# One core, two transformer blocks: the expert loop at the very end, the shift products beside the gate-up, the bias strip behind the gates, and the first projection from features that are not yet normed

## The chip, the cores and the metric

The kernel runs on one core of a Trainium2 chip. The metric is the device time of one execution in microseconds. Each kernel has a few timed runs, and one further execution is recorded by the hardware profiler; the rows below are of that execution.

## The reference, cut to what matters

The input is one sequence of 512 tokens with 1024 features in float32. Two blocks follow each other.

```python
# first block
h = rms_norm(x, g_mix)                      # x * rsqrt(mean x^2) * g
proj = h @ w_in                             # conv parts, q, k, v, iq, ik, iw, two gates
score = sum_h iw[t,h] * relu(iq[t,h] . ik[s])   # index scores, causal
idx = top_k(score, 128)                     # 128 keys for each query
logits = q.k * 64**-0.5 + rel_bias[bucket(t - s)]   # on the chosen keys
x = x + (sigmoid(g_a) * y_conv + sigmoid(g_b) * y_attn) @ w_out
x = x + (silu(h2 @ w_gate) * (h2 @ w_up)) @ w_down
x = rms_norm(x, g_final)
# second block
sh1, sc1, gt1, sh2, sc2, gt2 = split(silu(c) @ ada_w + ada_b)
h = rms_norm(x, g1) * (1 + sc1) + sh1
z = h @ w_in_2                              # latent q and kv, rope key, conv, gates
... latent attention, 31 tap convolution, gates, x = x + gt1 * y
h = rms_norm(x, g2) * (1 + sc2) + sh2
x = x + gt2 * moe(h)                        # 32 experts, 2 for each token
out = rms_norm(x, g_final_2)
```

## The kernel before

Activations stand with features on the partitions: x is 8 blocks (k = 0 to 7) of 128 features by 512 tokens. Nearly all matmuls are float32 products made from a high and a low part: `split` writes the high part on ScalarE and the rest on VectorE or GpSimd. `dense` (L351) runs a weight matrix chunk by chunk. For a chunk SyncE loads `raw` (512 KB, 8 blocks of 128 by 128), ScalarE makes `wh` (L338), GpSimd makes `wl` (L339), TensorE runs 24 matmuls (`mm3`: high by high, high by low, low by high for the 8 blocks) into one of three PSUM buffers `mm`, and an evacuation function takes the result. `raw`, `wh` and `wl` come from one ring of nine buffers. `dense` is a generator; `next(g)` emits one step, so other work is emitted between chunks. The order in each engine's queue is fixed when the program is built: a planner places the instructions by its own estimate of their times, with the order of emission as priority. An engine runs its queue in order, and SyncE issues its DMAs in order.

**First projection.** `w_qk` has ten chunks: index key (m = 0), index queries (1 to 4), key (5), queries (6 to 9). The first NDEF = 5 read `xg`, the features times `g_mix` without the norm, and `ev_qk` multiplies their products with the norm factor `r`, spread over the partitions (L511). Then `norm_h` (L499) makes all 8 blocks of `h` (L502, and a split whose low part is made by VectorE for even k and by GpSimd for odd k). `w_vi` (v and the index weights iw, 72 columns) and the chunks m = 5 to 9 read `h`. Scores (L549) for one query block and one index head are two matmuls, a relu on ScalarE and a multiply-add on VectorE, and are emitted four at a time between the chunks. `w_cv` (12 chunks) and the gates (`w_ga`, `w_gb`) read `h` as well. The top-k tasks (L562) run beside `w_cv`, `w_ga` and `w_ya`.

**Bias strip.** The bias by distance stands in DRAM as `bd` (8 by 640); one DMA writes from it `bt` (8 by 128 by 512, 2 MB, DRAM to DRAM, L645), emitted behind the last `w_cv` chunk. The attention reads it one head at a time (`st<-bt`, L766).

**Ada and shift.** The 48 loads of `ada` are reduced on VectorE, one scaled addition of 128 by 512 for each half (`ada`, L704), one task beside each chunk of the first half of gate-up and of down, two beside each chunk of the second gate-up half until the 54 tasks are used up. `shift` (L902) takes for each of the six chunks of `w_lat` a load of 512 KB, eight VectorE operations of 128 by 128 (L905, L907), one matmul with a column of ones (L909) and a copy. It runs beside the first six of the eight `w_dn` chunks of the second half (L964), where rope tables and masks are also made.

**Experts.** Seventeen tiles of rows (seq) go through the experts; sixteen of 112 rows and one of 64. Rows of tiles 0 to 14 are added to `acc` in DRAM by indirect DMAs, those of the last two (i = 15 and 16) stay on the chip and are placed with one-hot matmuls (`keep_on_chip`, `place`). `loop` (L1725) is a `tc.For_i(1, ntl)` loop for further tiles with a count read from `ei`. Here its count is one, so no iteration runs: the trace has 17 gathers. It is emitted inside the tile sequence at i = LOOP = 16, ahead of `turn(16)` and `finish(16)`. After it `fin` (4 blocks of tokens) is read from `acc`, `place` adds the kept rows, ScalarE sums the squares, and the last norm and the output follow.

Of the kernel before, what the change touches and what calls it, by code (L numbers as in the profile page):

```python
# [19 lines left out]
P = 128  # L20
# [29 lines left out]
FM = "ppss"  # L50
FQ = 1
KS = 0
NDEF = 5
SE = 0
CB = 48
FAR = 512.0
# [17 lines left out]
GA1 = (0, 0, 0, 1, 0, 1, 0, 1, 1, 0)  # L74
NW = 9
NCH = 2
LOOP = 16
LF = True
NX = 18
NR = 8  # L80
# [158 lines left out]
def build(tc, A, out, taps=None):  # L239
# [57 lines left out]
    def vcol(n, j, w=1):  # L297
        o = V1[n] + j
        return vec[:, o:o + w]
# [196 lines left out]
    next(g)  # L496
    h = []

    def norm_h():  # L499
        for k in range(DB):  # L500
            t = blk("t")
            STT(t, x[k], vcol("g_mix", k), r, ALU.mult, ALU.mult)  # L502
            a = pair_of("h")
            split(t, *a, eng=G if k % 2 else V)
            h.append(a)


    def ev_qk(m, ps):
# [15 lines left out]

    next(g)
    next(g)
    norm_h()
    go(g)
    g = dense("w_qk", DB, h, ev_qk, src=A["w_qk"][NDEF:], m0=NDEF)


    wh, wl = wsplit(wload(A["w_vi"].rearrange("p k c -> p (k c)"), 576), 576)
    ps = psum("mm", "vi")
    mm3(ps[:72], wh, wl, 0, DB, h, M=72)
    vi = blk("t")
    act(vi[:72], ps[:72], ACT.Copy)
    ps = psum("tp")
    for b in range(NB):
        nc.tensor.transpose(ps[:, b * 72:(b + 1) * 72], vi[:72, b * P:(b + 1) * P], ident[:72, :72])
# [40 lines left out]

    scores = Tasks(*[(score, b, i) for b in range(1, NB) for i in range(8)])
    scores.run(SC[0])
    go(g, lambda i: scores.run(SC[1]))
    scores.run(SC[2])
    tops = Tasks(*[(topk, b, j) for j in range(16) for b in range(1, NB)])

# [52 lines left out]
    def beside(i):  # L639
        scores.run(SC[3])  # L640
        if not scores.ts:
            tops.run(TOP)

    go(dense("w_cv", DB, h, ev_cv), beside)
    nc.sync.dma_start(bt, bass.AP(tensor=bd.tensor, offset=bd.offset + 127,  # L645
                                    ap=[[640, 8], [-1, P], [1, S]]))


    gts = {}
# [3 lines left out]
        act(t, ps, ACT.Sigmoid, bias=vcol("b_gate", m))  # L653
        gts[m] = t

    mA = []

    def ev_ya(m, ps):
        t = blk("mA")
        TT(t, ps, gts[m], ALU.mult)  # L660
        mA.append(t)

    ga, ya = dense("w_ga", DB, h, ev_ga), dense("w_ya", 4, chl, ev_ya)
    for _ in range(NGA):
        next(ga)
        tops.run(3)
        next(ya)
        tops.run(1)
    tops.run(99)

    gd = {}
# [227 lines left out]

    shc = kpool.tile([P, NL], F32, name="shc")  # L900

    def shift(c):  # L902
        raw = wload(A["w_lat"][c].rearrange("p m k c -> p (m k c)"), D)
        t = blk("t")[:, :P]
        TS(t, raw[:, :P], adac[:, :1], None, ALU.mult)  # L905
        for k in range(1, DB):
            STT(t, raw[:, k * P:(k + 1) * P], adac[:, k:k + 1], t, ALU.mult, ALU.add)  # L907
        ps = psum("lg", "shift")
        mm(ps[:, :1], t, one1[:, :1])  # L909
        act(shc[:, c:c + 1], ps[:, :1], ACT.Copy)  # L910

    shifts = Tasks(*[(shift, c) for c in range(NL)])


    gs1 = kpool.tile([P, 8], F32, name="gs1")
# [3 lines left out]
    for half in range(2):  # L919
        hid = []  # L920
        st = {}

        def ev_gu(m, ps):
            t = blk("t")
            if m % 2 == 0:
                TT(t, ps, r, ALU.mult)
                act(t, t, ACT.Silu)  # L927
                G.tensor_tensor(t, t, r, ALU.mult)  # L928
                st["g"] = t
            else:  # L930
                TT(t, ps, st["g"], ALU.mult)
                a = pair_of("h" if len(hid) < NH else "h1" if len(hid) < NH1 else "hid")
                split(t, *a)
                hid.append(a)

        if half == 0:
            with soon(1):
                r = rstd_of(ssq.done(), out=blk("m2"))
        if half == 0:
            keep(act(cact, vcol2("c", 0, 8), ACT.Silu))  # L940
            keep(G.tensor_copy(trib, cst[:, 256:384]))
            G.tensor_copy(tri2[:, :32], cst[:32, 256:288])
            G.tensor_tensor(tri2[:, 32:], cst[:32, 256:288], cst[:32, :32], ALU.add)
            G.tensor_copy(moeb, moec[:, 88:328])
            G.memset(oneb, 1.0)
        go(dense("w_gu", DB, h, ev_gu, src=A["w_gu"][half * 22:(half + 1) * 22]),
           lambda i: adas.run(AD[2 * half]))

        def ev_d(m, ps):
            TT(x[m], ps, x[m], ALU.add)  # L950
            if half:
                a = pair_of("xg")
                split(x[m], *a, scale=gs1[:, m:m + 1])
                xg.append(a)
                s1.add(x[m])
                s2.add(x[m], scale=vcol("g_final", m))

        if half:
            STT(gs1, adac[:, 8:16], 1.0, vcol2("norm1_g", 0, 8), ALU.add, ALU.mult)
            TT(gs1, gs1, vcol("g_final", 0, 8), ALU.mult)  # L960
            rt = rope_tables()
            mk = masks()
        go(dense("w_dn", 11, hid, ev_d, src=A["w_dn"][half]),
           lambda i: shifts.run(1) if half else adas.run(AD[2 * half + 1]))  # L964


    KQ = 96
# [754 lines left out]
        ohs.append(oh)  # L1722
        ys.append((yh, yl))

    def loop():  # L1725
        for j in range(LOOP + 1, 17):
            weights(j, LF)

        ntl = nc.values_load(ei[0:1, 16:17], min_val=1, max_val=16)
        with tc.For_i(1, ntl) as t:  # L1730
            st = mr[0].tile([P, 4], F32, name="lsl")[:, :3]

            nc.sync.dma_start(slots[16 * P:].rearrange("(g p) c -> p g c", p=P), slt[:, 16:])
            nc.sync.dma_start(st[:64], slots[bass.ds(16 * P + 64 * t, 64)])
            ix = mr[0].tile([P, 1], I32, name="lix")
            V.tensor_copy(ix[:64], st[:64, 0:1])
            w = further(t)
            xg = gather(xgb[0], ix, 64)
            scaled(64, xg, st)
            down(w, turned(64, hidden(w, features(64, xg, xtb), st)), yb[0])  # L1740
            add(64, yb[0], ix, acc)

    def rows_in_place(i):
        xts[i] = features(size(i), xgb[i % NQ], xtb)
# [16 lines left out]
    for i in range(17):  # L1761
        if i not in wes:
            weights(i)
        if i == 15:
            weights(16)
            gfr = xgb[i % NQ]
            keep(nc.sync.dma_start(gfr, A["gfin"].broadcast_to([P, D])))
        hss[i] = hidden(wes[i], xts.pop(i), slt[:, seq[i]], (lambda: turn(i - 1)) if i else None)
        if i < 16:
            rows_in_place(i + 1)  # L1770
        if i < 15:
            scaled(size(i + 2), xgb[(i + 2) % NQ], slt[:, seq[i + 2]])
        if i:
            finish(i - 1)
        if i == 0:
            further_tiles(further_slots())
        if i == LOOP:
            loop()
    turn(16)
    finish(16)  # L1780

    if LOOP == 17:
        loop()


    fin = []
    for b in range(NB):
        fin.append(mr[0].tile([P, D], F32, tag="we", bufs=NR, name="fin"))
        (nc.scalar if FQ and b % 2 else nc.sync).dma_start(fin[b], acc[b * P:(b + 1) * P])
# [21 lines left out]
    for b in range(2):  # L1811
        for q in range(2):
            placed(b, q, 0)

    for g in FGR:
        n = len(g)
        ms = mr[0].tile([P, n], F32, tag="ms%d" % n, bufs=2, name="ms")
        tg = {}
        for j, b in enumerate(g):
            place(b)  # L1820
            act(x_tile("sq"), fin[b], ACT.Square, accum_out=ms[:, j:j + 1])  # L1821
            if FM[b] != "s":
                tg[b] = mr[0].tile([P, D], F32, tag="we", bufs=NR, name="tg")
                (G if FM[b] in "pq" else V).tensor_tensor(tg[b], fin[b], gfr, ALU.mult)
        TS(ms, ms, 1.0 / D, EPS, ALU.mult, ALU.add)  # L1825
        r = rsqrt4(ms, lambda: mr[0].tile([P, n], F32, tag="rs%d" % n, bufs=6, name="rs"))
        for j, b in enumerate(g):
# [26 lines left out]
```

## Time and profile before

| what | value |
|---|---|
| timed runs | 1363.75, 1366.8 and 1368.21 us, median 1366.8 |
| profiled execution | 1365.68 us |
| its span, first to last instruction | 1363.9 us |
| TensorE busy | 1263.6 us (93%) in 5818 matmuls |
| VectorE, ScalarE, GpSimd busy | 845.9, 544.8, 645.7 us |
| mean granted TensorE clock | 0.964 of full speed |

Busy times are sums over the whole span; an engine can be the bound in one stretch and idle in another. A matmul of 512 columns is recorded with 0.39 us, but matmuls overlap: at full clock 16 of them take 3.79 us as a merged row.

### The profile page before, as it was taken

The numbers are of one execution on the slowest core, as the hardware profiler recorded it, in microseconds if no ns is written. First come the engines' busy times: TensorE is split into PE (matmuls) and PEld (weight loads), VectorE is DVE, ScalarE is ACT, GpSimd is POOL, SyncE is SP. The second block draws the span as 40 slices with busy tenths as digits, with TensorE's granted clock in tenths as the row PEclk, the third lists the DMA queues.
The fourth block names the chain that finished last, engine by engine and source line by source line (L and its number), as shares of the span: only waits on it lengthen the run. The fifth ranks groups of instructions, "written<-read, shape, count | busy, mean of one in ns | idle before, by whom it ended". The sixth has DMA issues, their size and how long they took to land. (4 is left out here: it accounts for less than half of the span.)

```text
span 1363.9 us, 16404 instructions
## 1 busy us (share of the span) xinstructions
PE 1263.6 (93%) x5818; PEld 946.5 (69%) x5818; DVE 845.9 (62%) x1490; ACT 544.8 (40%) x902; POOL 645.7 (47%) x365
## 2 busy tenths in 40 slices
PE   6798999999999999999998999899979999679985
PEld 5576887777888778777886777778855587445432
DVE  5857885543758443377249676979977753554424
ACT  4443236566333332222323454233376532244422
POOL 4514447454547554454745755346734263123311
PEclk9898999999999999999999999899989999879987
DMA  5214233223245544575333322234430069989983
GB/s 171 80 49 147 103 99 125 99 95 125 93 137 201 202 156 149 185 244 193 118 116 112 118 93 78 71 124 131 131 108 16 24 236 356 347 302 288 273 306 134
DMA packets 70403, 209.19 MB, mean 153 GB/s; under 512 B 9635, under 2 KB 14427, under 8 KB 70320
## 3 DMA queue, kind: packets, MB, share of 16 engines
q1 hardware_dynamic: 61456, 193.81, 41.4%
q0 software_dynamic: 4048, 8.01, 2.5%
q10 hardware_dynamic: 4816, 6.31, 1.3%
q8 instruction: 46, 0.75, 0.2%
q14 instruction: 37, 0.30, 0.1%
HBM read 195.06 MB, written 21.61 MB: 159 GB/s over the span
## 5 line engine op out<-in xcount | busy, mean ns | idle before, releaser
L339 POOL TENSOR_TENSOR wl<-raw,wh 128x1024 fp32r<-128x1024 f32 (+2 forms) x180 | 420.0, 2335 | 418.7 <-ACT wh L338 350.0
L338 ACT ACTIVATE wh<-raw 128x1024 fp32r<-128x1024 f32 (+2 forms) x183 | 183.3, 1003 | 297.8 <-DMA raw<-in_w_dn 59.3
L347 PE MATMUL pw_gu<-xg,wh 128*128 128x512 f32 x704 | 168.9, 391 | 0.0
L347 PEld LDWEIGHTS pw_gu<-xg,wh 128*128 128x128 f32 x704 | 131.4, 188 | 31.3 <-issue 2.5
L704 DVE SCALAR_TENSOR_TENSOR ad<-raw,cact,ad 128x512 f32<-128x512 f32 x84 | 89.0, 1107 | 37.1 <-DMA raw<-in_ada 37.1
L347 PE MATMUL pw_dn<-h,wh 128*128 128x512 f32 x352 | 88.6, 397 | 0.7 <-ACT wh L338 0.7
L347 PE MATMUL pw_cv<-h,wh 128*128 128x512 f32 x320 | 81.0, 405 | 8.0 <-ACT wh L338 5.0
L1048 DVE SCALAR_TENSOR_TENSOR ptaps<-u,vec,ptaps 128x511 f32<-128x511 f32 (+28 forms) x116 | 85.8, 739 | 3.6
L347 PE MATMUL pw_gu<-xg,wl 128*128 128x512 f32 x352 | 87.7, 390 | 0.0
L1639 PE MATMUL plg<-we,xt 128*64 128x256 f32 (+1 forms) x528 | 75.0, 406 | 9.2 <-DMA we<-in_we 6.0
L347 PEld LDWEIGHTS pw_cv<-h,wh 128*128 128x128 f32 x320 | 62.2, 196 | 23.6 <-ACT wh L338 5.9
L347 PEld LDWEIGHTS pw_dn<-h,wh 128*128 128x128 f32 x352 | 66.1, 190 | 15.6 <-ACT wh L338 1.2
L347 PEld LDWEIGHTS pw_gu<-xg,wl 128*128 128x128 f32 x352 | 65.9, 188 | 13.8
L1639 PEld LDWEIGHTS plg<-we,xt 128*64 128x64 f32 (+1 forms) x528 | 39.8, 136 | 40.2 <-issue 13.5
L347 PE MATMUL pw_gb<-h,wh 128*128 128x512 f32 x256 | 64.3, 394 | 0.0
L347 PE MATMUL pw_ga<-h,wh 128*128 128x512 f32 x256 | 62.3, 391 | 0.0
L347 PEld LDWEIGHTS pw_ga<-h,wh 128*128 128x128 f32 x256 | 47.7, 188 | 10.3 <-issue 0.8
L347 PEld LDWEIGHTS pw_gb<-h,wh 128*128 128x128 f32 x256 | 47.4, 188 | 9.2
L735 DVE TENSOR_SCALAR e<-e,ri 128x512 f32<-128x512 f32 (+2 forms) x64 | 49.0, 767 | 1.7
L928 POOL TENSOR_TENSOR t<-t,m 128x512 f32<-128x512 f32 x22 | 33.3, 1514 | 34.7 <-ACT t L927 32.7
L1600 POOL DMA_INDIRECT xg<-htok,sidx x17 | 17.2, 1012 | 67.2 <-ACT xt L1629 50.1
L733 ACT ACTIVATE e<-e,mx 128x512 f32<-128x512 f32 (+2 forms) x64 | 40.7, 637 | 20.1 <-DVE mx L776 13.2
(463 smaller groups left out, 2504.4 us busy)
## 6 DMA issues: line engine op xcount, KB each, us to landing
we<-in_we SPq DMA_DIRECT2D x99, 512.0 KB
raw<-in_ada SPq DMA_DIRECT2D x48, 512.0 KB
raw<-in_w_gu SPq DMA_DIRECT2D x44, 512.0 KB
raw<-in_w_cv SPq DMA_DIRECT2D x20, 512.0 KB
raw<-in_w_ga SPq DMA_DIRECT2D x16, 512.0 KB
raw<-in_w_gb SPq DMA_DIRECT2D x16, 512.0 KB
raw<-in_w_o SPq DMA_DIRECT2D x16, 512.0 KB
spill<-g SPq DMA_DIRECT2D x24, 256.0 KB
```

Of the source, the lines that this page charges most:

```text
L338: act(wh[:, :n], raw[:, :n], ACT.Copy)
L339: (eng or G).tensor_tensor(wl[:, :n], raw[:, :n], f(wh[:, :n]), ALU.subtract)
L347: mm(ps, w[:, o + k * M:o + (k + 1) * M], xs[k][i], start=(first and j == 0), stop=(last and j == n - 1))
L704: STT(t, raw[:, o], cact[:, k:k + 1], t, ALU.mult, ALU.add)
L733: act(e, e, ACT.Exp, scale=-1.0, bias=mx[:, h_, b:b + 1], accum_out=sm[:, h_, b:b + 1])
L735: (G if b in NP else V).tensor_scalar(e, e, r, None, ALU.mult)
L928: G.tensor_tensor(t, t, r, ALU.mult)
L1048: keep(STT((a if k else y)[:, s:], u[:, :S - s], w, a[:, s:], ALU.mult, ALU.add))
L1600: rows_in.append(keep(nc.gpsimd.indirect_dma_start(out=xg[:n], out_offset=None, in_=htok, in_offset=bass.IndirectOffsetOnAxis(ap=si_[:n], ...
L1639: keep(mm(pg[64 * j:min(64 * j + 64, n), :256], xt[:, k, 64 * j:min(64 * j + 64, n)], w[k // 4][:, k % 4 * 256:(k % 4 + 1) * 256], start=( ...
```

## The change

1. `NDEF = 10`: all ten chunks of `w_qk` read `xg`, and `ev_qk` multiplies each with `r`. `norm_h` makes one block of `h` at a time: three beside chunks 2 to 4, the rest beside chunks 5 to 9. `w_vi` reads `xg` too, and its copy on ScalarE becomes a multiplication with `r` on VectorE.
2. The DMA of the bias strip is emitted behind the first four pairs of `w_ga` and `w_ya` chunks, and may be issued only after the first `ev_ya`.
3. `shift` runs beside the second half of gate-up, from the chunk on in which no `ada` task is left; the matmul and copy of column c are emitted in the task of c + 1, so there are seven tasks. Beside `w_dn` of the second half there is nothing.
4. The loop is emitted after `place` and the sums of squares and ahead of the last norm; the count is read ahead of the loads of `fin`. The body of the loop no longer adds its rows to `acc` but makes one-hot rows, splits, 16 matmuls and additions to `fin`, and makes the sums anew.

```diff
-NDEF = 5
+NDEF = 10
-LOOP = 16
...
-    def norm_h():
-        for k in range(DB):
-            t = blk("t")
-            STT(t, x[k], vcol("g_mix", k), r, ALU.mult, ALU.mult)
-            a = pair_of("h")
-            split(t, *a, eng=G if k % 2 else V)
-            h.append(a)
+    def norm_h(k):
+        t = blk("t")
+        STT(t, x[k], vcol("g_mix", k), r, ALU.mult, ALU.mult)
+        a = pair_of("h")
+        split(t, *a, eng=G if k % 2 else V)
+        h.append(a)
...
-    norm_h()
-    go(g)
-    g = dense("w_qk", DB, h, ev_qk, src=A["w_qk"][NDEF:], m0=NDEF)
+    for k in range(3):
+        next(g)
+        norm_h(k)
...
-    mm3(ps[:72], wh, wl, 0, DB, h, M=72)
+    mm3(ps[:72], wh, wl, 0, DB, xg, M=72)
     vi = blk("t")
-    act(vi[:72], ps[:72], ACT.Copy)
+    TT(vi[:72], ps[:72], r[:72], ALU.mult)
...
-    go(g, lambda i: scores.run(SC[1]))
+    for k in range(3, DB):
+        next(g)
+        scores.run(SC[1])
+        norm_h(k)
+    for _ in g:
+        scores.run(SC[1])
...
     go(dense("w_cv", DB, h, ev_cv), beside)
-    nc.sync.dma_start(bt, bass.AP(tensor=bd.tensor, offset=bd.offset + 127,
-                                    ap=[[640, 8], [-1, P], [1, S]]))
...
-        TT(t, ps, gts[m], ALU.mult)
+        strip.append(TT(t, ps, gts[m], ALU.mult))
...
         tops.run(1)
+    with tc.issue_after(strip[0].ins):
+        nc.sync.dma_start(bt, bass.AP(tensor=bd.tensor, offset=bd.offset + 127,
+                                        ap=[[640, 8], [-1, P], [1, S]]))
...
+    sht = {}
+
     def shift(c):
+        if c > 0:
+            ps = psum("lg", "shift")
+            mm(ps[:, :1], sht[c - 1], one1[:, :1])
+            act(shc[:, c - 1:c], ps[:, :1], ACT.Copy)
+        if c == NL:
+            return
         raw = wload(A["w_lat"][c].rearrange("p m k c -> p (m k c)"), D)
-        t = blk("t")[:, :P]
+        t = sht[c] = blk("t")[:, :P]
         TS(t, raw[:, :P], adac[:, :1], None, ALU.mult)
         for k in range(1, DB):
             STT(t, raw[:, k * P:(k + 1) * P], adac[:, k:k + 1], t, ALU.mult, ALU.add)
-        ps = psum("lg", "shift")
-        mm(ps[:, :1], t, one1[:, :1])
-        act(shc[:, c:c + 1], ps[:, :1], ACT.Copy)
-
-    shifts = Tasks(*[(shift, c) for c in range(NL)])
+    shifts = Tasks(*[(shift, c) for c in range(NL + 1)])
...
-           lambda i: adas.run(AD[2 * half]))
+           lambda i: adas.run(AD[2 * half]) if adas.ts else shifts.run(1))
...
-           lambda i: shifts.run(1) if half else adas.run(AD[2 * half + 1]))
+           lambda i: None if half else adas.run(AD[1]))
...
-    def loop():
-        for j in range(LOOP + 1, 17):
-            weights(j, LF)
-
-        ntl = nc.values_load(ei[0:1, 16:17], min_val=1, max_val=16)
+    def loop(ntl, ms, tg):
         with tc.For_i(1, ntl) as t:
...
-            add(64, yb[0], ix, acc)
+            yh, yl, oh = raw_tile("yh", F32R), raw_tile("yl", F32R), raw_tile("oh", F32R)[:, :S]
+            for b in range(NB):
+                TS(oh[:64, b * P:(b + 1) * P], it128[:64], float(P * b), st[:64, 0:1], ALU.add, ALU.is_equal)
+            for q in range(2):
+                o = slice(q * S, (q + 1) * S)
+                split(yb[0][:64, o], yh[:64, o], yl[:64, o])
+            for b in range(NB):
+                for q in range(2):
+                    o, ps = slice(q * S, (q + 1) * S), psum("mm")
+                    for i, y in enumerate((yh, yl)):
+                        mm(ps, oh[:64, b * P:(b + 1) * P], y[:64, o], start=(i == 0), stop=(i == 1))
+                    TT(fin[b][:, o], ps, fin[b][:, o], ALU.add)
+                sums(b, ms, tg)
...
-        if i == LOOP:
-            loop()
     turn(16)
     finish(16)
...
     fin = []
+    ntl = nc.values_load(ei[0:1, 16:17], min_val=1, max_val=16)
...
+        for b in g:
             place(b)
+            sums(b, ms, tg)
+        loop(ntl, ms, tg)
         TS(ms, ms, 1.0 / D, EPS, ALU.mult, ALU.add)
```

## Rows read from the trace of the kernel before

**Rows 1.** The span in 40 equal slices, from the page, in tenths.

```profile
PE   6798999999999999999998999899979999679985
...
PEclk9898999999999999999999999899989999879987
```

**Rows 2.** Waits of PE over the span: us in total, times, longest.

```profile
PE pvi L347 <- DVE t L511: 7.3, 1, 7.3
PE pshift L909 <- DVE t L907: 7.3, 5, 3.4
...
PE pw_cv L347 <- ACT wh L338: 5.0, 2, 4.8
```

**Rows 3.** Busy time by stretch: us, PE, PEld, DVE, ACT, POOL, PEclk, DMA share, GB/s.

```profile
35.00:57.00 22.00, 14.01 (x58) 11.02 (x59) 21.78 (x21) 11.29 (x18) 14.23 (x8) 0.86 0.21 68
57.00:97.00 40.00, 39.69 (x179) 30.27 (x178) 20.19 (x29) 16.76 (x34) 7.28 (x3) 0.99 0.14 43
```

**Rows 4.** Timeline of PE, 44 to 63 us: start, us, what, [idle before].

```profile
54.61 4.61 PE L347 MATMUL pvi<-h,wh 128*72 128x512 f32 x13 [7.27 <-DVE t L511]
59.05 2.23 PE L347 MATMUL pw_qk<-h,wh 128*128 128x512 f32 x9
```

**Rows 5.** Groups of DVE, 35 to 57 us: count, busy us, mean ns, idle before.

```profile
L502 DVE SCALAR_TENSOR_TENSOR t<-x,vec,s 128x512 f32<-128x512 f32 x8 | 8.8, 1144 | 0.0
...
L309 DVE TENSOR_TENSOR h<-t,h 128x512 fp32r<-128x512 f32 x4 | 4.7, 1174 | 0.1
L511 DVE TENSOR_TENSOR t<-pw_qk,s 128x512 f32<-128x512 f32 x5 | 3.2, 681 | 4.8 <-ACT s L436 4.8
```

**Rows 6.** Timeline, 84 to 130 us: SP, ACT and PE around the strip.

```profile
95.73 0.79 SPq L645 DMA_DIRECT2D bt<-bd  x1
...
96.64 28.73 SPq L333 DMA_DIRECT2D raw<-in_w_cv  x6
...
110.18 1.06 ACT L338 ACTIVATE wh<-raw 128x1024 fp32r<-128x1024 f32 x1 [4.47 <-DMA raw<-in_w_cv]
...
111.28 5.99 PE L347 MATMUL pw_cv<-h,wh 128*128 128x512 f32 x16 [4.79 <-ACT wh L338]
```

**Rows 7.** Timelines of DVE, SP and PE, 184 to 210 us.

```profile
185.76 0.67 DVE L660 TENSOR_TENSOR mA<-pw_ya,g 128x512 f32<-128x512 f32 x1
...
189.42 12.04 SPq L333 DMA_DIRECT2D raw<-in_w_gb  x3
...
206.45 3.79 PE L347 MATMUL pw_gb<-h,wh 128*128 128x512 f32 x16
```

**Rows 8.** Busy time of the second half of down, columns as in Rows 3.

```profile
703.10:778.07 74.97, 66.54 (x277) 52.57 (x276) 63.92 (x94) 26.43 (x44) 43.93 (x28) 0.95 0.39 126
```

**Rows 9.** Timeline of PE in the first half of down: starts of two chunks.

```profile
529.26 2.88 PE L347 MATMUL pw_dn<-h,wh 128*128 128x512 f32 x12
...
536.75 2.88 PE L347 MATMUL pw_dn<-h,wh 128*128 128x512 f32 x12
```

**Rows 10.** Costliest groups over the span, from the page.

```profile
L339 POOL TENSOR_TENSOR wl<-raw,wh 128x1024 fp32r<-128x1024 f32 (+2 forms) x180 | 420.0, 2335 | 418.7 <-ACT wh L338 350.0
...
L928 POOL TENSOR_TENSOR t<-t,m 128x512 f32<-128x512 f32 x22 | 33.3, 1514 | 34.7 <-ACT t L927 32.7
```

**Rows 11.** Line L907: duration min, median, max in ns.

```profile
L907 DVE SCALAR_TENSOR_TENSOR t<-raw,adac,t x42: 338/352/1932, 728.1 to 769.8; 128x128 f32<-128x128 f32 x42
```

**Rows 12.** Groups of DVE in two stretches: 605 to 650 us, 727 to 770 us.

```profile
L704 DVE SCALAR_TENSOR_TENSOR ad<-raw,cact,ad 128x512 f32<-128x512 f32 x22 | 27.8, 1323 | 0.0
...
L907 DVE SCALAR_TENSOR_TENSOR t<-raw,adac,t 128x128 f32<-128x128 f32 x42 | 29.7, 728 | 0.9
```

**Rows 13.** Chain that ended last, in order of time: start, us, what.

```profile
1335.14 0.07 issue
...
1337.17 0.69 DVE y L1668
...
1351.66 1.16 ACT sq L1821 x2
```

More of the change, by code (lines that the diff above doesn't have):

```diff
@@ L654, in ev_ga @@
         gts[m] = t
-    mA = []
+    mA, strip = [], []
     def ev_ya(m, ps):
         t = blk("mA")
-        TT(t, ps, gts[m], ALU.mult)
+        strip.append(TT(t, ps, gts[m], ALU.mult))
         mA.append(t)
@@ L1776, in build @@
             further_tiles(further_slots())
-        if i == LOOP:
-            loop()
     turn(16)
     finish(16)
-    if LOOP == 17:
-        loop()
     fin = []
+    ntl = nc.values_load(ei[0:1, 16:17], min_val=1, max_val=16)
     for b in range(NB):
@@ L1813, in build, with sums @@
             placed(b, q, 0)
+    def sums(b, ms, tg):
+        act(x_tile("sq"), fin[b], ACT.Square, accum_out=ms[:, b:b + 1])
+        if b in tg:
+            (G if FM[b] in "pq" else V).tensor_tensor(tg[b], fin[b], gfr, ALU.mult)
     for g in FGR:
@@ L1817, in build @@
         ms = mr[0].tile([P, n], F32, tag="ms%d" % n, bufs=2, name="ms")
-        tg = {}
-        for j, b in enumerate(g):
+        tg = {b: mr[0].tile([P, D], F32, tag="we", bufs=NR, name="tg") for b in g if FM[b] != "s"}
+        for b in g:
             place(b)
[L1821 to L1824, printed above, removed]
+            sums(b, ms, tg)
+        loop(ntl, ms, tg)
         TS(ms, ms, 1.0 / D, EPS, ALU.mult, ALU.add)
```

## The prediction

> **What bounds the kernel now.** I began with the 40 slices [rows 1]: TensorE stands at 9 in 30 of them, so most of the span is one engine's work back to back, and only the slices with a lower digit can give time. Three groups of these concern the change: slices 0 to 3, slice 21 (counted from 0), and slices 38 and 39 at the end. The others are not touched. Then I read who holds TensorE up [rows 2]. Three of its long waits lie in places that the diff edits: 7.3 us at `pvi` for a VectorE evacuation, 7.3 us in five waits at the shift matmuls, 5.0 us at `w_cv` for a weight chunk. Every microsecond below is one in which TensorE stood still or ran at its lower clock; work that is merely moved beside a full TensorE counts nothing.
>
> **First projection.** TensorE stood from 47.3 to 54.6 us, 7.27 us [rows 4]. What it waited for is VectorE, busy for 21.78 of the 22 us from 35 to 57 [rows 3]: all eight blocks of h are made there in one go, 8.8 us for the scaled copies and 4.7 us for the low parts of four blocks [rows 5], ahead of evacuations that TensorE needs to have a PSUM buffer free. The granted clock over that stretch is 0.86 on average, the lower level in part of it: behind the gap 13 matmuls take 4.44 us (54.61 to 59.05), where a chunk of 33 takes 7.49 us at full clock [rows 9], 0.227 us each or 2.95 us for 13. So gap and slow start cost 7.27 + 1.49 = 8.8 us.
>
> The change takes five of the eight blocks out of the stretch: 8.8 x 5/8 = 5.5 us and half of the low parts, 2.35 us, together 7.9 of VectorE's 21.78 us; it adds one multiplication for v, 0.68 us. That leaves 14.6 of 22. The 7.9 us go to the 40 us behind, where VectorE is busy for 20.19, and five multiplications with r of 0.681 us [rows 5] come along: 20.2 + 7.9 + 3.4 = 31.5 of 40. Both stretches are then under the time that TensorE needs, and no matmul up to `w_cv` reads h. The gain lies between nothing (if VectorE's fixed order puts other things first) and 8.8 us. I leave 1.5 us for waits, two evacuations of 0.68 us queued ahead of the one that TensorE needs: **minus 7.3 us**. What is late next is the last block of h, emitted behind the last chunk; four scores and the first `w_cv` matmuls lie ahead of its use. The copy that leaves ScalarE costs nothing there, since ScalarE has 11.29 busy of 22 us.
>
> **Bias strip.** Issued at 95.73 us, it stands ahead of the `w_cv` load of 96.64, whose data ScalarE gets at 110.18: 13.5 us. TensorE waits 4.79 us, and its next 16 matmuls take 5.99 us [rows 6] where 3.79 are usual [rows 7], 2.20 more. The move gives back 4.79 + 2.20 = 7.0 us, if the strip costs nothing where it goes. There it may start when the first `ev_ya` ends at 186.4 us, and SyncE issues a `w_gb` load 3 us later, at 189.42 [rows 7]. If that takes 13.5 us too it is there at 202.9; with 1.06 us for the high part [rows 6] and 2.34 for the low [rows 10] the chunk is ready at 206.3, and TensorE wants it at 206.45 [rows 7]. So the cover is just long enough (all three times move forward alike). Bounds: nothing, and the same 7.0 us lost again; by the sum I take 0.5: **minus 6.5 us**. Behind the waiting DMA stand only weight loads and the strips of the first head.
>
> **Shift.** The second half of down takes 74.97 us, VectorE busy for 63.92 of it [rows 8]. In the first half a chunk starts 7.49 us after the one before [rows 9]; eight are 59.9 us. The difference, 15.1 us, is what goes on beside it. Rope tables and masks stay, and so do the splits; I leave 1.4 us, twice an evacuation, for them. The six loads of 512 KB and the 48 VectorE operations go to gate-up, where a chunk of 24 matmuls is 24 x 0.227 = 5.45 us. A shift is eight operations: 2.8 us at the 0.352 of the median [rows 11], 5.8 us at the mean of 0.728 [rows 12]. With about 1.1 us of evacuation and split, VectorE needs 3.9 to 6.9 us for a chunk of 5.45. At 6.9 six chunks fall behind by 8.7 us; the matmul now waits one chunk longer, which covers 5.45, so 3.3 us are lost, at 3.9 nothing. The nearest row is ada in the same stage: four additions in each chunk at a mean of 1.323 us [rows 12], 5.3 us a chunk, and TensorE stays at 9 there (slices 17 and 18 [rows 1]). Two loads a chunk for ada become one, so the ring and the queue of SyncE are no worse off. I take 2.0 us. Sum: 15.1 - 1.4 - 2.0, **minus 11.7 us**.
>
> **Loop.** With no iteration the loop costs its entry and exit: the chain that ended last is held on VectorE's semaphores from 1335.14 to 1337.17 [rows 13], 2.0 us between the two halves of tile 15's result. That goes. At the new place the same steps stand between the last square of ScalarE, which ends at 1351.66 + 1.16 = 1352.82 us, and the norm. No row shows it there, nor the jump over a longer body. Bounds: nothing, and all of 2.0. The other engines are done earlier and can pass most of their semaphores while ScalarE works, so I take 0.8: **minus 1.2 us**. The early read of `fin` is worth nothing, since the placing waits for tile 16.
>
> **Sum.** 7.3 + 6.5 + 11.7 + 1.2 = 26.7 us. The profiled execution took 1365.7 us, so 1339.0; the median of the runs lies 1.1 us above it, which makes 1340.1. What lies behind each place shifts forward alike, since loads there are released by buffers that TensorE frees.
>
> **Rivals.**
> *VectorE becomes the bound of gate-up.* The operations of a shift wait for GpSimd: 0.352 us at the median, 0.728 on average [rows 11, 12]. If the planner puts the deferred matmul so close behind its operations that the slack is gone, all 8.7 us are lost instead of 2.0: 1346.8. For it: slice 21, where just that happens. Against it: ada. The Trainium skill ("SBUF — State Buffer", section "Who interferes with whom") says that a VectorE instruction with two SBUF inputs and a GpSimd one that reads SBUF exclude each other for their whole length; the mean of twice the median agrees. By that rule alone a chunk would take 2.34 + 1.51/2 for GpSimd, 8 x 0.352 for the shift and some 0.45 for half a split, 6.4 us in all; six times 0.92 over 5.45 is 5.5 us, the slack used up, and the time between 1340 and 1343.6.
> *VectorE stays the bound of the first projection.* The evacuations stand behind norms and scores in its fixed order and TensorE waits as long as now: 7.3 us less gain, 1347.4. For it: 21.78 of 22 [rows 3]; against it: the 7.9 us that leave.
> *The strip holds up the gates.* It costs 7.0 us again: 1346.6. For it: a margin of 0.15 us; against it: the loads stand two chunks ahead of their use.
> *The time is given back later.* The expert stretch at the end is fed by the DMAs; if its loads did not start earlier with the rest, its waits would grow by what was gained: 1366.
> *Slower.* The shift operations wait for GpSimd far longer in gate-up. To lose all 26.7 us and 0.3% more (4.1 us), gate-up must lose 2.0 + 30.8 = 32.8: six chunks of 11.8 us less the slack, which is 10.7 us a shift or 1.34 us for each operation. The mean is 0.728, the longest 1.932 [rows 11]. At 1.6 us for each the time would be 1383.
>
> **How the numbers follow.** My forecast 0.62; gate-up bound by VectorE 0.13; first projection still bound 0.10; strip 0.06; given back 0.05; slower 0.04. The likeliest gives 1340. With every bound at its good end the gain is 8.8 + 7.0 + 15.1 + 2.0 = 32.9 and the time 1333.9; some slow-clock time behind the loop's gap that I did not count makes 1330 the low end. One of the first three rivals gives at most 1347.4, two of them in part 1352: the high end. What is outside is the last two rivals and two full ones together. A measurement here can tell about 0.3% (4 us) from no change. Faster by more: 0.62 + 0.13 + 0.10 + 0.06 = 0.91; within: 0.05; slower by more: 0.04.
>
> **What would show it.** Right: no wait over 2 us at `pvi` or between 36 and 95 us; the second `w_cv` chunk without a gap behind the first; the second half of down near 61 us and no wait at the shift matmuls; VectorE straight from tile 15's first half to its second; no clock fall in these places. Wrong: TensorE waiting for VectorE in the last ten gate-up chunks or at the projection's evacuations, for a `w_gb` chunk behind the strip, or more than 1 us of semaphores between the last square and the norm.

## The result and the profile after

The runs of the changed kernel have a median of 1351.5 us (1347.1 to 1354.8), those of the kernel before beside them 1366.1: a ratio of 0.988, with a 95% interval of 0.986 to 0.991. The forecast was 1340 with a range up to 1352. So the change is faster, by 14.6 us where 26.7 were forecast, and the result lies half a microsecond inside the high end. The profiled execution took 1354.8 us with a span of 1353.0, 10.9 us shorter than the span before.

The 40 slices of the changed kernel, which answer to [rows 1]:

```profile
PE   6988999999999999999999999899979999679885
...
PEclk8998999999999999999999999899979999889987
```

Slice 1 (counted from 0) went from 7 to 9 and slice 21 from 8 to 9: the first projection, and the shift's share leaving down. Slice 2, 68 to 101 us, went from 9 to 8. The windows say more (us, PE, PEld, DVE, ACT, POOL, clock, DMA share, GB/s):

```profile
24.00:34.00 10.00, 9.37 (x31) 7.76 (x32) 4.94 (x18) 0.00 (x0) 0.00 (x0) 0.66 0.16 52
35.00:57.00 22.00, 20.46 (x96) 15.77 (x95) 18.05 (x18) 13.14 (x20) 12.56 (x6) 1.00 0.35 109
57.00:92.00 35.00, 34.25 (x158) 26.98 (x156) 21.40 (x32) 13.42 (x27) 6.71 (x4) 1.00 0.11 34
92.00:112.00 20.00, 12.29 (x36) 7.96 (x37) 19.41 (x25) 11.26 (x19) 8.73 (x5) 0.74 0.52 184
660.00:690.00 30.00, 27.26 (x122) 22.05 (x121) 28.96 (x44) 8.02 (x15) 15.55 (x8) 0.97 0.42 138
708.60:768.30 59.70, 59.70 (x265) 49.44 (x264) 36.42 (x46) 26.37 (x39) 43.51 (x27) 1.00 0.35 112
```

Against [rows 3] the projection is full now: 20.46 of 22 us where TensorE had 14.01. Against [rows 8] the second half of down takes 59.7 us in place of 74.97. But from 92 to 112 us TensorE works 12.29 of 20 us at a clock of 0.74, and from 660 to 690 us VectorE is busy for 28.96 of 30. The timelines (start, us, what, idle before) say why, first at the start of `w_cv`:

```profile
91.13 0.79 SPq L671 DMA_DIRECT2D bt<-bd  x1
92.04 5.27 SPq L332 DMA_DIRECT2D raw<-in_w_cv  x3
...
98.94 0.74 DVE L500 SCALAR_TENSOR_TENSOR t<-x,vec,s 128x512 f32<-128x512 f32 x1
...
105.70 0.75 DVE L500 SCALAR_TENSOR_TENSOR t<-x,vec,s 128x512 f32<-128x512 f32 x1
...
92.21 1.66 PE L346 MATMUL pw_cv<-h,wh 128*128 128x512 f32 x6 [0.27 <-ACT wh L337]
...
100.40 0.50 PE L346 MATMUL pw_cv<-h,wh 128*128 128x512 f32 x1 [2.80 <-ACT h L307]
...
107.14 8.85 PE L346 MATMUL pw_cv<-h,wh 128*128 128x512 f32 x29 [3.33 <-ACT wh L337]
```

Two things are late here. The strip's DMA still goes out at 91.13 us, ahead of a `w_cv` load: in [rows 6] it was 95.73 and 96.64. The edit did not move it. And six of the sixteen first matmuls are through when block 6 of h is missing; it is scaled at 98.94 us and block 7 at 105.70, after the scores, the low parts of q and the first top-k steps that stand ahead of them on VectorE.

The shift's matmul in gate-up, one chunk behind its operations, and VectorE at the end of the program:

```profile
687.23 0.38 PE L912 MATMUL pshift<-one,t 128*128 128x1 f32 x2 [2.74 <-DVE t L920]
687.47 1.43 PE L346 MATMUL pw_gu<-xg,wh 128*128 128x512 f32 x4
688.70 3.35 PE L346 MATMUL pw_gu<-xg,wl 128*128 128x512 f32 x8
```

```profile
1323.08 1.52 DVE L1678 TENSOR_TENSOR y<-pmm,gt2r 112x512 f32<-112x512 f32 x2 [0.25 <-PE pmm L1677]
1324.52 0.68 DVE L308 TENSOR_TENSOR yl<-y,yh 112x512 fp32r<-112x512 f32 x1
1325.12 0.86 DVE L1726 TENSOR_SCALAR oh<-moeb,slt 64x128 fp32r<-64x128 bf16 x4
1325.90 0.68 DVE L308 TENSOR_TENSOR yl<-y,yh 112x512 fp32r<-112x512 f32 x1
1326.50 0.21 DVE L1668 COPY ht<-ptp 128x64 f32<-128x64 f32 x1
```

The same place on VectorE before, with the loop between the halves:

```profile
1334.30 0.69 DVE L1668 TENSOR_TENSOR y<-pmm,gt2r 112x512 f32<-112x512 f32 x1 [0.25 <-PE pmm L1667]
1337.17 0.69 DVE L1668 TENSOR_TENSOR y<-pmm,gt2r 112x512 f32<-112x512 f32 x1 [2.18 <-ACT yh L308]
1337.78 0.21 DVE L1658 COPY ht<-ptp 128x64 f32<-128x64 f32 x1
```

And the chain of the changed kernel between the last square and the norm:

```profile
1341.92 0.04 DVEq L1737
1341.96 0.16 issue
1342.12 0.18 DVE ms L1844
```

After the wait of 2.74 us eight matmuls take 3.35 us where 1.98 are usual. The two halves of tile 15's result now follow each other without semaphores (1.52 us for both), yet the copy `ht` for tile 16 comes 3.42 us after the first half; before it came 3.5 us after, behind the second half directly (1334.30 and 1337.78). The last square ended at 1341.15 us, and the norm starts at 1342.12.

### The profile page after: what moved, and what is told of

The parts are those of the page before. It is cut to its first block, busy times and chain, and to the rows that moved or that the text cites. A ratio compares the mean times of both kernels' runs of the same rounds, so it can differ in the third digit from the quotient of the medians.

```text
span 1353.0 us, 16405 instructions
## 1 busy us (share of the span) xinstructions
PE 1262.8 (93%) x5818; PEld 947.5 (70%) x5818; DVE 850.0 (63%) x1496; ACT 544.1 (40%) x901; POOL 642.7 (48%) x365
## 5 line engine op out<-in xcount | busy, mean ns | idle before, releaser
L346 PE MATMUL pw_dn<-h,wh 128*128 128x512 f32 x352 | 85.4, 390 | 0.0
L1649 PEld LDWEIGHTS plg<-we,xt 128*64 128x64 f32 (+1 forms) x528 | 39.9, 137 | 39.0 <-issue 12.9
```

The costliest lines, as they stand in the source:

```text
L346: mm(ps, w[:, o + k * M:o + (k + 1) * M], xs[k][i], start=(first and j == 0), stop=(last and j == n - 1))
L1649: keep(mm(pg[64 * j:min(64 * j + 64, n), :256], xt[:, k, 64 * j:min(64 * j + 64, n)], w[k // 4][:, k % 4 * 256:(k % 4 + 1) * 256], start=( ...
```

## The stages of all runs

Each trace was cut at the first and last matmuls of the same groups, in us: when `w_cv` starts; from there to the first `w_ga` and on to the first `w_yb`; gate-up from its first to its last matmul (the first half of down lies in it); from there to the first `w_lat`, which is the second half of down; and from the last matmul to the end of the span. The medians and ratios are of all timed runs, each against the kernel before on the same chip. The medians of the kernel before lay between 1366.1 and 1369.1 us beside these runs, so kernels are compared by their ratios. Left out, besides the experts themselves, are the stretch from the first `w_yb` to gate-up (71.4 us in all traces but two, 72.9 with the strip held in the kernel before and with the parts on SyncE) and that from the first `w_lat` to the first product of the experts, where no edit lies: it takes 432.7 to 438.9 us, and no run shows why it differs by up to 6 us.

| kernel | w_cv starts | to w_ga | to w_yb | gate-up | down 2 | end | median | ratio, 95% |
|---|---|---|---|---|---|---|---|---|
| before | 97.4 | 76.4 | 144.3 | 313.8 | 74.8 | 13.1 | 1366.1 | |
| after | 92.2 | 80.7 | 144.4 | 320.0 | 59.7 | 13.8 | 1351.5 | 0.988 (0.986 to 0.991) |
| before, projection alone | 89.2 | 80.6 | 144.3 | 313.8 | 73.8 | 12.6 | 1360.7 | 0.994 (0.992 to 0.996) |
| before, strip held | 97.5 | 68.6 | 150.7 | 313.8 | 73.8 | 13.0 | 1366.7 | 0.999 (0.998 to 1.001) |
| before, shift alone | 98.9 | 77.0 | 144.3 | 317.8 | 59.7 | 12.7 | 1354.2 | 0.989 (0.987 to 0.991) |
| after, loop back | 90.5 | 80.7 | 144.3 | 320.2 | 59.7 | 13.0 | 1350.8 | 0.987 (0.985 to 0.989) |
| after, strip held | 90.8 | 81.0 | 147.7 | 320.3 | 59.7 | 13.9 | 1353.9 | 0.990 (0.988 to 0.992) |
| after, h early | 89.1 | 77.7 | 144.3 | 320.3 | 59.7 | 13.9 | 1349.3 | 0.987 (0.985 to 0.989) |
| both | 90.5 | 68.6 | 152.4 | 317.8 | 59.7 | 13.5 | 1346.9 | 0.984 (0.982 to 0.986) |
| after, matmul two back | 89.2 | 81.1 | 144.3 | 320.0 | 59.7 | 14.0 | 1348.9 | 0.986 (0.984 to 0.987) |
| the same, held | 89.1 | 81.0 | 144.4 | 316.6 | 59.7 | 14.0 | 1349.0 | 0.985 (0.983 to 0.987) |
| h early, strip in parts on SyncE | 88.8 | 89.6 | 155.1 | 320.5 | 59.7 | 13.0 | 1370.5 | 1.002 (1.001 to 1.004) |
| h early, parts on ScalarE | 88.8 | 68.6 | 147.5 | 320.2 | 59.7 | 13.0 | 1340.8 | 0.982 (0.980 to 0.984) |
| all that helped | 89.4 | 68.6 | 147.7 | 317.8 | 59.7 | 13.1 | 1338.9 | 0.979 (0.977 to 0.982) |

## The experiments

**The start of `w_cv`: strip, late h, or both.** The strip's DMA was given a dependence of its own on the first product of the gates, so that SyncE waits for it:

```diff
-    with tc.issue_after(strip[0].ins):
-        nc.sync.dma_start(bt, bass.AP(tensor=bd.tensor, offset=bd.offset + 127,
-                                        ap=[[640, 8], [-1, P], [1, S]]))
+    late_bt = nc.sync.dma_start(bt, bass.AP(tensor=bd.tensor, offset=bd.offset + 127,
+                                            ap=[[640, 8], [-1, P], [1, S]]))
+    tc.add_manual_dep(late_bt.ins, strip[0].ins.name, mybir.DependencyInfo(
+        mybir.DependencyClass.Sync, mybir.DependencyReason.DATA), reason="strip behind the gates")
```

> The kernel after, with the bias strip's DMA really held until the first product of the gates (a dependence of the DMA itself); in the trace after it still went out at 91.13 us, ahead of the w_cv load of 92.04. Theory (strip and late last blocks of h both bind the start of w_cv): the second w_cv chunk's data come some 10 us earlier, but TensorE still waits for h blocks 6 and 7 (100.4 and 107.0 us), so the start of w_ga moves by 0 to 2 us of 172.95 and the time is 1350 to 1351.5 by the same measure by which the kernel after has 1351.5. Rival one (the strip alone binds): w_ga starts 6 to 9 us earlier, 1343 to 1346. Rival two, of the prediction (the strip holds up the gates at its new place): a wait of 3 us or more at a w_gb chunk behind 190 us; by the prediction's sum it costs 0.5 us.

Blocks 3 to 7 of h were made earlier:

```diff
-    for k in range(3, DB):
-        next(g)
-        scores.run(SC[1])
-        norm_h(k)
+    for ks in ((3, 4), (5, 6), (7,)):
+        for k in ks:
+            norm_h(k)
+        next(g)
+        scores.run(SC[1])
```

> The kernel after, with the blocks 3 to 7 of h made two a chunk, ahead of the scores, from the sixth chunk of the first projection on; the strip as in the kernel after. Theory (both bind): chunk 0 of w_cv runs through before 103 us, but the second chunk's weights still come at 107 us; gained are the 17 matmuls of chunk 0 that lay behind 107 us, 17 x 0.227 = 3.9 us: 1347 to 1349. Rival one (the strip alone binds): no change, 1351.5. Rival two (the late h alone binds): 8 to 10 us, 1342 to 1344.

And both edits together:

> Both edits together: strip held, h early. Theory (both bind): w_cv runs through from 92 us, waits of 2.80 and 3.33 us and the low clock from 101 to 111 us are gone, the start of w_ga moves from 172.95 to 162 to 165, the time is 1341 to 1344, more than the sum of the two edits alone. Rival one (strip alone): as e1, 1343 to 1346 for both. Rival two (late h alone): as e2, 1342 to 1344 for both. A third (something else holds the start of w_cv, the scores beside it): less than 5 us, 1347 or more.

From the start of `w_cv` to that of `w_ga` the kernel after takes 80.7 us, with the strip held 81.0, with h early 77.7, with both 68.6: 12.1 us for both where the single edits give minus 0.3 and 3.0. That is what two causes that bind at the same time look like. The time with both, 1346.9 us, missed the 1341 to 1344 expected, by what follows. With both, TensorE works for all of the 20 us from 92 to 112 at full clock. With h early alone the wait for the weights behind the strip stayed, and grew (6.1 us, where it is 3.33 in the kernel after and 4.79 before):

```profile
PE pw_cv L346 <- ACT wh L337: 6.3, 2, 6.1
```

But with the strip held the next stage is longer, by 3.3 us alone and 8.0 us with both, and the time of the run with the strip held, 1353.9 us where 1350 to 1351.5 were expected, is not better than that of the kernel after. SyncE's timeline with the strip held, and GpSimd's and TensorE's behind it:

```profile
184.52 0.79 SPq L670 DMA_DIRECT2D bt<-bd  x1
187.38 18.30 SPq L332 DMA_DIRECT2D raw<-in_w_gb  x3
205.73 0.43 SPq L771 DMA_DIRECT2D st<-bt  x1
206.25 0.60 SPq L332 DMA_DIRECT2D raw<-in_w_gb  x1
...
210.18 2.37 POOL L338 TENSOR_TENSOR wl<-raw,wh 128x1024 fp32r<-128x1024 f32 x1 [4.86 <-ACT wh L337]
212.52 2.10 POOL L780 TENSOR_TENSOR e<-st,mk 128x128 f32<-128x128 f32 x3
...
213.36 0.44 PE L777 MATMUL plg<-q 128*128 128x384 f32 x1 [1.98 <-DVE mx L781]
```

The fetch of the first head's bias `st` stands in the queue until the strip is there, 21 us after its issue, and a `w_gb` load stands behind the fetch. GpSimd, which adds bias and mask for the first logits, stands idle for 4.86 us ahead of the split of such weights at 210.18 and comes to the bias at 212.52; TensorE waits 1.98 us for the logits. With both edits that wait is 2.6 us, and the granted clock from 198 to 218 us is 0.91.

**The strip alone in the kernel before** has the same edit:

> The kernel before, with the bias strip alone really held until the first product of the gates (before, h is complete when w_cv starts). Prediction: 7.0 us less in front of the second w_cv chunk, 0.5 us lost at the new place, 6.5 us faster. Theory from the runs with the strip held: the w_cv stage gives the 7 us (76.4 to about 69.5 us up to w_ga), but the strip lands some 20 us late for the first head's logits, 3 to 5 us lost between w_ga and w_yb (144.3 us in the kernel before), and VectorE's top-k is reached by TensorE: net 1 to 4 us faster. Rival (as the prediction): 6 us or more.

It gains 7.8 us up to `w_ga` (68.6 in place of 76.4), loses 6.4 on the way to `w_yb` and 1.5 more from there to gate-up: no change that can be told. Two waits of TensorE for this stretch:

```profile
PE plg L774 <- DVE mx L778: 2.7, 1, 2.7
PE pw_ga L347 <- DVE t L634: 1.7, 1, 1.7
```

The second is for VectorE's product for the last `w_cv` chunk. VectorE, with the top-k beside, is busy for 56.96 of the 60 us from 112 to 172 and does not follow when TensorE is earlier. Another 1.0 us of waiting for VectorE comes at `w_ya`. So of the 6.4 us these 2.7 are not the strip's. With both edits the waits at `w_ga` and `w_ya` are 1.7, 1.0 and 0.5 us, 3.2 of the 8.0, and a further wait of 2.2 us stands at `w_yb`, for ScalarE's part of the attention.

**The projection alone in the kernel before**, with nothing else changed:

> The kernel before, with the edits of the first projection alone (ten index chunks from the unnormed features, v from them too, h one block a chunk); strip, shift and loop as before. Prediction: 7.3 us faster. Theory from the runs so far: w_cv starts 8 us earlier than the 97.4 of the kernel before (5 where the low clock comes behind the features' wait at 25 us), but blocks 6 and 7 of h are late for it and the strip still stands ahead of its second chunk, so that from the start of w_cv to that of w_ga it takes 80 to 81 us in place of 76.4: 4 us faster, 1 where the low clock comes. Rival (late h costs nothing without the other edits): 7 to 8 us faster, 76 to 77 us from w_cv to w_ga.

`w_cv` starts 8.2 us earlier, and it then takes 80.6 us to `w_ga`, as in the kernel after. So 4.0 us are left, where the kernel after, with the later start behind its low clock, has 0.9. The time fell by more, 8.4 us. The trace does not show the rest; the profiled execution of before, 1365.7 us, is below the medians of 1366.1 to 1369.1 that its runs had beside the experiments, so I rest on the stages and not on the difference of one span.

**The shift.** Alone in the kernel before:

> The kernel before, with the move of the shift's share alone (its operations beside the last chunks of gate-up, its matmul one chunk behind). Prediction: 11.7 us faster. Theory from the two traces: the second half of down goes from 75.0 to 59.9 us as in the kernel after (15.1 us), the second half of gate-up loses 6.2 us, so 8.9 us faster, within a microsecond. Rival (the stall of gate-up is made by what the other edits moved): gate-up loses 2 us or less, 13 us faster.

Down gives 15.1 us as in the kernel after. Gate-up loses 4.0 us here and 6.2 there; the wait is 2.27 us here, and no clock fall follows. By its medians it is 13.2 us faster, where 8.9 were expected and the whole change gives 14.6. The three parts alone add up to 13.2 + 8.4 + 1.2 = 22.8 us by their medians. One trace of each kernel shows 5.2 us that bear on the difference: in the kernel after `w_cv` starts 3.0 us later than with the projection alone, and gate-up is 2.2 us longer than with the shift alone, each behind a clock fall that the other trace does not have. The rest stays open, and which of the timed runs have these falls is not recorded.

Then the matmul two chunks behind its operations:

```diff
-        if c > 0:
+        if c > 1:
...
-            mm(ps[:, :1], sht[c - 1], one1[:, :1])
+            mm(ps[:, :1], sht[c - 2], one1[:, :1])
...
-    shifts = Tasks(*[(shift, c) for c in range(NL + 1)])
+    shifts = Tasks(*[(shift, c) for c in range(NL + 2)])
```

> The kernel after, with the matmul of each shift two chunks behind its VectorE operations instead of one, so that the last falls one chunk later; the work is the same. Theory (gate-up loses its 6.2 us at the matmul: a wait of 2.74 us, 1.7 us of low clock behind it, the rest the twelve small matmuls themselves): the wait and the clock fall go, gate-up ends 4.4 us earlier, 1347. Rival (VectorE, busy 9.6 to 9.7 of 10 us there, holds up the evacuations of gate-up instead, as the operations that wait for GpSimd last 2.3 us): TensorE waits for a PSUM buffer in place of the shift matmul, 1350.5 to 1351.5.

Gate-up is as long as before the edit, 320.0 us. The fixed order put the shift's matmuls 2 to 4 matmuls later than in the kernel after, and only the last one nine; it seems that the planner takes an instruction where it expects its data. VectorE, GpSimd and TensorE of this run:

```profile
677.73 7.61 DVE L920 SCALAR_TENSOR_TENSOR t<-raw,adac,t 128x128 f32<-128x128 f32 x7
...
687.43 1.89 DVE L920 SCALAR_TENSOR_TENSOR t<-raw,adac,t 128x128 f32<-128x128 f32 x5
...
678.25 1.39 POOL L938 TENSOR_TENSOR t<-t,m 128x512 f32<-128x512 f32 x1 [2.65 <-ACT t L937]
679.59 4.83 POOL L338 TENSOR_TENSOR wl<-raw,wh 128x1024 fp32r<-128x1024 f32 x2
691.09 2.41 POOL L338 TENSOR_TENSOR wl<-raw,wh 128x1024 fp32r<-128x1024 f32 x1 [6.66 <-ACT wh L337]
...
685.40 0.38 PE L912 MATMUL pshift<-one,t 128*128 128x1 f32 x2 [1.95 <-DVE t L920]
```

Seven additions take 7.61 us while GpSimd works almost through, five take 1.89 us while it is idle. The Trainium skill ("SBUF — State Buffer", section "Who interferes with whom") has a VectorE instruction with two inputs in SBUF contend with a GpSimd one that reads SBUF, for a pair of ports that one of them locks. The trace agrees, with 1.09 against 0.38 us an addition. The same with the matmul held by a dependence on the evacuation of the chunk ahead of it:

```diff
...
+            m = mm(ps[:, :1], sht[c - 2], one1[:, :1])
+            tc.add_manual_dep(m.ins, evs[-1].ins.name, mybir.DependencyInfo(
+                mybir.DependencyClass.Sync, mybir.DependencyReason.DATA), reason="shift behind a chunk")
...
```

> As the deferral by two chunks, with each shift matmul held by a dependence on the evacuation of a chunk between; in the run before this one the fixed order put the matmul back to 1 to 3 matmuls from its old place, and gate-up took 320.0 us as in the kernel after. Now it stands 7 matmuls (1.6 us) later than there. Theory (the loss of gate-up is the wait at the matmul and the clock fall behind it): the wait of 1.95 us goes to under 0.5, no clock fall, gate-up 316 to 317 us, the time 3 to 4 us under that of the kernel after. Rival (VectorE, held up by GpSimd, makes the evacuations late anyway): 319 us or more, and TensorE waits elsewhere in the last chunks.

Gate-up takes 316.6 us, 3.4 less, and no clock fall follows. But the wait is still there:

```profile
PE pshift L913 <- DVE t L944: 1.1, 1, 1.1
```

It is now for the evacuation (L944) that the edit ties the matmul to, no longer for the additions. So a later matmul shortens the wait, from 2.74 and 1.95 us to 1.1, not to the 0.5 or less that was expected. The rest of the 3.4 us goes with the clock fall, and no run shows that the held matmul removes that: with both edits the matmul is not held, the wait is 2.24 us, there is no fall, and gate-up takes 317.8 us. The rival's wait for a PSUM buffer stands in no trace. The timed runs do not tell the two apart, 0.986 and 0.985 of the kernel before.

**The loop back** at its place of before, in the kernel after:

> The kernel after, with the loop back at its place of before, between the two halves of tile 15's result, and its old body; all else as in the kernel after. Prediction: 1.2 us slower than the kernel after. Theory from the two traces (0.5 us gained at tile 16, 0.8 to 1.2 us lost at the end, between the last square and the norm): 0.3 to 0.7 us faster than the kernel after, less than the runs tell; in the trace some 2 us of semaphores stand between the halves of tile 15 again, and the norm follows the last square without them. Rival (the loop at the end hides wholly behind ScalarE): 2 us slower.

The time is 1350.8 us, the intervals overlap. VectorE stands idle for 2.18 us between the halves of tile 15 again. In the chain of waits the norm follows the last square with 0.02 us between:

```profile
1337.57 1.16 ACT sq L1833 x2
1338.72 0.02 issue
1338.75 0.18 DVE ms L1837
```

From the last matmul to the end it is 12.6 to 13.1 us in the six traces with the loop at its old place (mean 12.9) and 13.0 to 14.0 in the eight with it at the end (mean 13.6).

**Another place for the strip.** Four DMAs of two heads, first on SyncE's queue, each with a dependence on an evacuation of `w_cv`, in chunks 1, 3, 5 and 7:

> h early, and the bias strip in four DMAs of two heads, each held until one more pair of w_cv chunks is done, so that none stands long ahead of a weight load and all are there before the gates. In the run with both edits the w_cv stage gave 12.1 us, but 8.0 us were lost again between the start of w_ga and that of w_yb. Theory (of the 8.0 us the strip, landed 21 us after its issue beside the w_gb loads, costs 4 to 5 through the first head's logits; the rest is VectorE's top-k, which now ends later than TensorE wants it): w_cv to w_ga 68 to 70 us, w_ga to w_yb 147 to 148 us, some 4 to 5 us under the run with both edits. Rival one (the whole loss is the top-k's): w_ga to w_yb 152 us again, no better than both edits. Rival two (a part ahead of a w_cv load holds TensorE up each time): w_cv to w_ga over 73 us.

A miss, by the second rival of the expectation: 89.6 us from `w_cv` to `w_ga`, and slower than the kernel before.

```profile
128.06 0.63 SPq L645 DMA_DIRECT2D bt<-bd  x1
128.78 4.60 SPq L332 DMA_DIRECT2D raw<-in_w_cv  x2
149.22 0.60 SPq L645 DMA_DIRECT2D bt<-bd  x1
...
142.42 1.06 ACT L337 ACTIVATE wh<-raw 128x1024 fp32r<-128x1024 f32 x1 [13.44 <-DMA raw<-in_w_cv]
...
149.34 5.57 PE L346 MATMUL pw_cv<-h,wh 128*128 128x512 f32 x16 [8.48 <-DVE t L638]
```

A part waits for an evacuation, the next weights wait behind the part in the queue, and ScalarE waits for the weights ahead of the next evacuation: a ring of waits of 21.2 us for two chunks (128.06 to 149.22) that need 10.9. Then the same parts on ScalarE's queue, each behind an evacuation that ScalarE itself makes:

```diff
...
+    def strip_part(m, ins):
+        if m in (1, 3, 6, 7):
+            i = 2 * (1, 3, 6, 7).index(m)
+            with tc.issue_after(ins.ins):
+                nc.scalar.dma_start(bt[i:i + 2], bass.AP(tensor=bd.tensor, offset=bd.offset + 127 + 640 * i,
+                                                         ap=[[640, 2], [-1, P], [1, S]]))
...
```

> h early, and the strip in four DMAs of two heads on ScalarE's queue, each behind an evacuation of ScalarE's own in w_cv (chunks 1, 3, 6, 7), so that nothing on the queue of the weight loads waits. The four parts held on the queue of the weight loads made each load behind them late, 89.6 us from w_cv to w_ga. Theory: w_cv to w_ga 68.5 to 71 us as with both edits (68.6), w_ga to w_yb 147 to 148 us where both edits had 152.4, as the strip is there in time and only the top-k is left; 4 to 5 us under the run with both edits, 1342 where before has 1367. Rival one (the top-k of VectorE makes the whole loss): w_ga to w_yb 152 us again, 1346. Rival two (the parts slow the weight loads whatever queue they stand on): w_cv to w_ga over 73 us.

This holds the DMA without a wait on the queue of the weights: 68.6 us to `w_ga`, and 147.5 to `w_yb`, 4.9 less than with both edits. What waits are left there are for VectorE at `w_ga` and `w_ya`, 1.5 and 1.0 us, and for ScalarE at `w_yb`, 2.2. All that helped together:

> All that helped together: h early, the strip in four parts on ScalarE's queue, the shift matmuls held behind a chunk, the loop at its place of before. By the theory the run before it (1342 where before has 1367) less 3.4 us of gate-up and 0.8 us behind the last square: 1337 to 1339. Rival (what is gained ahead is lost again at the top-k or in the expert stretch): 1342 or more.

Its median is 1338.9 us, 0.979 of the kernel before where the kernel after has 0.988: the lowest of all, though its interval overlaps that of the run before it (0.980 to 0.984). Gate-up takes 317.8 us in it, 2.4 less than there, with a wait of 1.3 us for 2.24 and no clock fall; since it is 317.8 with both edits too, where no matmul is held, the 2.4 us are not shown to be the held matmul's. Of the 3 to 4 us from `w_lat` to the experts by which this trace and the one before it are shorter than that of the kernel after, no edit is shown to be the cause.

## Why the prediction was right in its sign and half wrong in its size

**First projection, minus 7.3 forecast.** The size was right where it was made: `w_cv` starts 8.2 us earlier in the kernel before with this part alone. It was 5.2 in the profiled execution of the kernel after, where the clock was low from 26 us. The step that failed is the one costed at nothing, that the last block of h is late but covered by four scores and the first `w_cv` matmuls. Blocks 6 and 7 came 8 and 15 us after `w_cv` had started, and 4.3 us were given back before `w_ga`. With h early 3.0 of them returned; the other 1.3 are the longer wait behind the strip, 6.1 us in place of 4.79.

**Bias strip, minus 6.5.** The step that failed first is that the move takes place. `issue_after` names an instruction of VectorE, and the DMA on SyncE's queue was issued at the same point of the order as before; on ScalarE's queue, behind an instruction of ScalarE, it did hold. That the change does nothing there was not among my rivals. Truly moved, it gives more in front (7.8 for 7.0), but the 0.5 us lost at the new place was 3.3 with the strip held in the kernel after, and 4.9 between both edits and the parts on ScalarE: the rival in which the strip holds up the gates, through the first head's logits and not through the first `w_gb` chunk. The 6.4 us of the kernel before hold 2.7 us of waiting for VectorE besides, which no rival had. I asked when the loads are late, and not who reads the strip next and what stands behind that reader.

**Shift, minus 11.7.** Down gave 15.1 us, and nothing of the 1.4 us that I left for it was lost. Gate-up lost 6.2 where I took 2.0, and that is the mis-sized term. It priced the wait alone, which was 2.74 us. The 1.4 us of low clock in the eight matmuls behind it and the twelve small matmuls that moved along were put at nothing; the stage of the shift alone, where no fall follows, has 4.0 - 2.27 = 1.7 us beside its wait. The mechanism of the wait is that of the rival with VectorE as the bound. The operations were not longer than I had assumed, 0.66 us on average for 0.728, with the same median of 0.352 (min, median, max in ns):

```profile
L920 DVE SCALAR_TENSOR_TENSOR t<-raw,adac,t x42: 341/352/2576, 654.0 to 690.8; 128x128 f32<-128x128 f32 x42
```

But from the first shift to the fifth their first operations start 6.4 us apart (653.67 to 679.29 us) where TensorE takes 5.7 us a chunk, and the fifth, with three operations of 1.27 to 2.37 us, needs 7.9 us, so the slack of one chunk was used up there. Ada was the wrong row to lean on: no matmul waits for its additions chunk by chunk, and the 22 of [rows 12] take 27.8 of 45 us, 3.4 us a chunk and not 5.3, which leaves VectorE pauses to catch up in. From 660 to 690 us it was busy for 28.96 of 30.

**Loop, minus 1.2.** The 0.8 us at the new place was right (0.97 us between the last square and the norm). The 2.0 us at the old place were worth nothing: three operations of VectorE, 0.68 + 0.86 + 0.68 us, moved ahead of the copy that tile 16 waits for and took the place of the semaphores.

**Sum.** In the profiled spans: minus 5.2 and plus 4.3 at the start, plus 6.2 in gate-up, minus 15.1 in down, minus 1.4 between `w_lat` and the experts, which no edit explains, and about nothing at the end, 10.9 in all. "Given back later" did not come: from `w_ga` on, gate-up and the end are the only stages that grew. That the result lies inside the range is luck as far as the terms go: its high end stood for two rivals in part, and what came is a strip that did not move, a late h that was put at nothing, a loop that gained nothing and a gate-up that lost three times its price.

## What to carry to other kernels

When two things bind the same wait, removing either shows little of what both are worth (minus 0.3 and 3.0 of 12.1 us here): look for the second cause before costing a removal, and test both together. Ask of each DMA that is moved which queue it waits on, who reads it first, and what stands behind that reader; a wait put on the queue that feeds the weights cost more here than the transfer had cost at its old place. A gap of semaphores is a gain only if what follows is next in line.

## What the runs showed of the hardware

TensorE's clock fell or did not after the same wait. Behind a wait of 2.3 us for the unnormed features at 24 us, the granted clock from 24 to 34 us was 0.66 in the kernel after, a mix of full speed (2.4 GHz) and half of it; with h early the wait was 2.2 us and the clock 1.00:

```profile
24.00:34.00 10.00, 9.31 (x47) 7.90 (x48) 5.01 (x18) 1.06 (x1) 0.77 (x1) 1.00 0.20 58
```

Among the traces that have the edit of the first projection, `w_cv` starts at 90.5 to 92.2 us in those with the fall and at 88.8 to 89.4 in the others; no edit decides it. The same in gate-up: a fall after 2.74 us (after), 2.24 (parts on ScalarE) and 1.95 (matmul two back), none after 2.24 (both) and 2.27 (shift alone). By these starts and stages each of the two places is worth some 2 us of a single trace, an estimate, and a stage cut from one trace has to be read with its clock.
